# An encoder trunk on one Trainium2 core: half-height score products, turned group-0 values, query norms inside the softmax, and elementwise work taken off GpSimd

## The chip, the core and the metric

The kernel runs on one core of one Trainium2 chip. The metric is the device time of one execution in microseconds (us). The engines are named as in the profile: PE is TensorE with PEld for its weight loads, DVE is VectorE, ACT is ScalarE, POOL is GpSimd, SP is SyncE, which here only issues DMAs. The median of three runs of the kernel before is 1399.47 us (1397.34 to 1400.84).

## What is computed

Two encoder layers work on 512 tokens of 1024 channels, all in float32. One layer, cut to what matters here:

```python
h    = layer_norm(x) * (1 + sc1) + sh1
proj = h @ w_in                       # q,k,v of branch A; q,k,v of branch B; two gates
# A: 8 query heads, 2 key heads, rms-normed per head, rotary; softmax over all 512 keys
qa = rope(rms_norm(qa, qn_g)); ka = rope(rms_norm(ka, kn_g))
out_a = softmax(qa @ ka.T / 8) @ va
# B: three groups of 4 heads, (window, dilation) = (128,1), (512,4), (2048,16), ALiBi bias
o_g, lse_g = dilated_group(qd, kd, vd)          # within the window, every dilation-th key
out_b = sum_g softmax_g(lse_g) * o_g
mix  = (g_a * (out_a @ w_pa) + g_b * (out_b @ w_pb)) @ w_o
x    = layer_norm(ALPHA * x + g1 * mix) * ln1_g + ln1_b
h2   = layer_norm(x) * (1 + sc2) + sh2
x    = layer_norm(ALPHA * x + g2 * moe(h2)) * ln2_g + ln2_b   # 16 experts, top 2 of the best group
```

## The kernel before

Tokens are worked on in four tiles of 128. Products of activations and weights take three passes (`gemm3`, L220): each operand is split into a rounded part H and a remainder L, and H*H, H*L and L*H are added. Weights come by SP's queue; `wsplit` (L195) makes H by an ACT copy (L215) and L by a DVE subtraction (L216). The products of attention and some transposes take plain float32, which stands in the trace as two PE instructions for a product. Each engine runs its instructions in a fixed order that a scheduler draws up at compile time, near the order of the program, with what it expects to be ready first.

The stages of a layer, with their place in layer 0 of the trace:

- Head (to 60 us): the modulation vectors, the normed input turned to channels-first, and its split `apply` (L372): four of eight remainders on POOL (L378). In layer 1 the head is `head_next` (L390), run tile by tile behind the end of layer 0; there POOL makes the remainder of block 3 (L413).
- Rope (94 to 119 us): `rope` (L588) squares and sums the queries and keys of a tile, POOL raises ten sums to the power -1/2 (`pool_rsqrt`, L286), DVE multiplies all 640 columns by the result (L604), ACT and DVE split them, PE turns them (`qk_trans`, L615). Between two tiles stands one product of `fill_b`.
- Branch A (126 to 264 us): 64 units of one head and one tile: score product (L647), maximum (L650), exponential (L653), four transposes, the value product. `fill_b` (L506) puts the projections for branch B between units. The values of group 0 are made there token-major (L527): five blocks of tokens, 24 products of 256 columns each. Those of groups 1 and 2 are made channels-first with 512 columns and turned later by `turned` (L552).
- Branch B (264 to 371 us): 24 units (group, pair of heads `ii`, tile `b`). `b_keys` (L727) copies the keys of two heads by SP's queue into a buffer whose other halves are zero, so that one full-height product (L743) gives both heads' scores. Bias (L745), maximum (L746), exponential (L749), transposes, copy and value product (`b_out`, L753) follow two units later. `fill_g` puts the gate projections in between, one at every second unit.
- Merge (392 to 433 us): `join` (L886), products with w_branch_a and w_branch_b, gating; POOL adds two of four blocks (L916).
- Out (433 to 495 us): `out_block` (L941): output projection by 256 columns, DVE scales (L947), POOL adds into `xr` but for two blocks (L948). `tile_x1` and `tile_h2` norm each tile twice through `norm` (L313): DVE works on 768 columns (896 for h2), ACT and POOL on the others. The h2 of the last tile is finished by ACT and POOL behind the router's sigmoid (L1003 to L1008) and stored by SP's queue.
- Router (495 to 517 us): a chain of small DVE instructions ranks the experts (L1011 to L1076), then POOL gathers token rows by an indirect DMA (`x_load`, L1102) into buffers `xe` that POOL zeroed (L1100).
- Experts (517 to 692 us): 16 experts, `x_gate`, `x_up`, `x_down`.
- Combine (from 692 us): `rows_in` (L1299) adds the experts' rows to x1: four of eight by an ACT scaling (L1303) and a POOL addition (L1304), the others by DVE (L1306). `combine` and `finish` norm each tile (L1341).

Of the kernel before, what the change touches and what calls it, by code (L numbers as in the profile page):

```python
# [87 lines left out]
def build(tc, A, out):  # L88
    nc = tc.nc
    with ExitStack() as es:  # L90
# [222 lines left out]
        def norm(src, name, g, b, st=None, cut=None):  # L313

            cut = cut or CUT
            m, r, nb = st or stats(src)
            n = f4(name, [D])
            for p, z in parts(src, cut, D) if cut < D else []:
                issued["act"] = ACT.activation(n[:, z], p, AF.Identity, bias=nb, scale=r)  # L319
            for p, z in parts(src, 0, cut):  # L320
                V.scalar_tensor_tensor(n[:, z], p, m, g[:, z], op0=OP.subtract, op1=OP.mult)  # L321
            a, z = slice(0, cut), slice(cut, D)
            issued["dve"] = V.scalar_tensor_tensor(n[:, a], n[:, a], r, b[:, a], op0=OP.mult, op1=OP.add)  # L323
            if cut < D:
                PO.tensor_tensor(n[:, z], n[:, z], g[:, z], op=OP.mult)  # L325
                PO.tensor_tensor(n[:, z], n[:, z], b[:, z], op=OP.add)
            return n
# [21 lines left out]
        def head_first(xt):  # L349
# [24 lines left out]
            def apply(k):  # L374
# [3 lines left out]
                (PO if k % 2 else V).tensor_tensor(L, z, H.bitcast(F32), op=OP.subtract)  # L378
# [11 lines left out]
        def head_next(l):  # L390
# [4 lines left out]
            def tile_in(t, x, st):  # L395
# [3 lines left out]
                for q in range(2):  # L399
# [10 lines left out]
                    for j in range(2 * q, 2 * q + 2):  # L410
                        f, H, L = F[:, 2 * j:2 * j + 2, :], hH[j][:, :, tcols(t)], hL[j][:, :, tcols(t)]
                        ACT.copy(H, f)  # L412
                        i = (PO if j in HLP else V).tensor_tensor(L, f, H.bitcast(F32), op=OP.subtract)  # L413
                        if j not in HLP:
                            issued["head"] = i
# [14 lines left out]
        def layer(l, hH, hL, W0, after=None, qk=None):  # L430
# [75 lines left out]
            def fill_b():  # L506
                for g in range(3):
# [16 lines left out]
                    if g == 0:  # L524
                        dst5 = small("vB5", [256], bufs=1)
                        turned()
                        for b in range(5):  # L527
                            p = pmm([P, 256])
                            lo, hi = max(0, P * b - 64), min(S, P * b + 64)
                            m = hi - lo  # L530
                            gemm3(p[0:m, :], range(8), lambda k: hcol(k, slice(lo, hi)), lambda k: W(k, slice(0, 256)))
                            ACT.copy(dst[0:m, b, :] if b < 4 else dst5[0:m, :], p[0:m, :])
                            if b % 2 == 1:
                                yield
                        vB.append((dst, dst5))
                    else:
                        for c in range(2):
                            turned()
                            p = pmm([P, S])
                            gemm3(p, range(8), lambda k: W(k, slice(c * P, (c + 1) * P)),  # L540
                                  lambda k: hcol(k, slice(0, S)))
                            vT = sc("vT", [S])
                            ACT.copy(by_tile(vT, g), by_class(p, g))
                            late.append((vT, dst, c))
                            yield
                        vB.append((dst, None))
# [5 lines left out]
            def turned():  # L552

                while late:
                    vT, dst, c = late.pop(0)
                    p = ptp([P, 4, P])
                    transposes(lambda b: vT[:, tcols(b)], p, 4)
                    V.tensor_copy(dst[:, :, c * P:(c + 1) * P], p)

# [26 lines left out]
            QK = {}  # L586

            def rope(t):  # L588
# [15 lines left out]
                V.tensor_mul(hv(a), hv(a), rs[:, :, None].to_broadcast([P, 10, HD]))  # L604
# [39 lines left out]
            def a_scores(h, t):  # L644
# [5 lines left out]
                V.tensor_reduce(nm, s, axis=X, op=OP.max, negate=True)  # L650
# [73 lines left out]
            for z in kz:  # L724
                PO.memset(z, 0.0)
# [687 lines left out]
```

## Time and profile before

| | us |
|---|---|
| median of three runs | 1399.47 |
| profiled execution | 1398.57 |
| span of its trace | 1396.8 |
| PE busy | 1278.9 |
| DVE busy | 1024.2 |
| ACT busy | 720.2 |
| POOL busy | 282.4 |

A timeline row gives start, duration, engine, line, operation, tile written and tiles read, shape, count, and in brackets the idle time before it with what ended it. Instructions of PE overlap: the pitch, from one start to the next, is what a product costs, not its duration. A row of a table of stretches gives the length, busy time and count for each engine, the granted TensorE clock, the DMA share and GB/s. A row of groups gives busy time and mean ns of one.

### The profile page before, as it was taken

What the parts mean: (1) busy time and instruction counts of PE and PEld (TensorE: products, weight loads), DVE (VectorE), ACT (ScalarE), POOL (GpSimd) and SP (SyncE); (2) the same over time, 40 slices, a digit from 0 to 9 for tenths busy, and PEclk for the clock granted to TensorE, in tenths of its full rate; (3) what the DMA queues carried; (4) which work ended last, traced back from release to release, by engine and by line L of the source; (5) the groups of instructions that cost most, each with busy time, mean ns of one, the idle gap of its engine ahead of it and who ended that gap; (6) DMA issues with size and microseconds to landing.
All of it is one profiled execution on the core that took longest, in us unless ns stands there. A gap on an engine that the chain in (4) does not pass through costs nothing. (4 is left out here: it accounts for less than half of the span.)

```text
span 1396.8 us, 21644 instructions
## 1 busy us (share of the span) xinstructions
PE 1278.9 (92%) x7953; PEld 1039.7 (74%) x7953; DVE 1024.2 (73%) x1974; ACT 720.2 (52%) x1506; POOL 282.4 (20%) x273
## 2 busy tenths in 40 slices
PE   5898999999998949999889999999999894999986
PEld 4797777677777938888659787767777784888862
DVE  5877777767367778999798877564336767899985
ACT  2344444555644237777645444455565522777760
POOL 1132000000002651221341300000000256222224
PEclk9999999999999969999999999999999996999998
DMA  9646654556155187999653555122214536799952
GB/s 317 218 156 239 208 167 167 154 185 218 32 174 204 61 272 260 308 346 338 233 182 125 160 181 170 61 76 76 76 46 151 180 122 218 272 301 344 352 206 84
DMA packets 182992, 266.76 MB, mean 191 GB/s; under 512 B 18665, under 2 KB 131721, under 8 KB 182880
## 3 DMA queue, kind: packets, MB, share of 16 engines
q1 hardware_dynamic: 159312, 225.46, 48.4%
q0 software_dynamic: 11456, 24.07, 4.9%
q10 hardware_dynamic: 12112, 15.78, 3.7%
q8 instruction: 64, 1.05, 0.3%
q14 instruction: 48, 0.39, 0.1%
HBM read 250.79 MB, written 27.30 MB: 199 GB/s over the span
## 5 line engine op out<-in xcount | busy, mean ns | idle before, releaser
L216 DVE TENSOR_TENSOR wL<-raw,wH 128x512 fp32r<-128x512 f32 x520 | 349.9, 703 | 67.3 <-ACT wH L215 52.0
L215 ACT CAST wH<-raw 128x512 fp32r<-128x512 f32 x520 | 318.9, 622 | 148.4 <-PE mm L1175 41.6
L225 PE MATMUL mm<-hH,wH 128*128 128x512 f32 x512 | 206.4, 403 | 0.0
L226 PE MATMUL mm<-hL,wH 128*128 128x512 f32 x512 | 202.4, 395 | 0.0
L227 PE MATMUL mm<-hH,wL 128*128 128x512 f32 x512 | 202.0, 394 | 0.0
L225 PE MATMUL mm<-wH,xH 128*128 128x256 f32 x512 | 149.1, 291 | 1.0 <-ACT xH L343 1.0
L227 PE MATMUL mm<-wH,xL 128*128 128x256 f32 x512 | 148.9, 291 | 0.9 <-DVE xL L344 0.9
L226 PE MATMUL mm<-wL,xH 128*128 128x256 f32 x512 | 146.6, 286 | 0.3 <-DVE wL L216 0.3
L249 DVE SCALAR_TENSOR_TENSOR acc<-araw,cond,acc 128x512 f32<-128x512 f32 x148 | 110.7, 749 | 5.5 <-DMA araw<-in_w_ada 2.3
L227 PEld LDWEIGHTS mm<-hH,wL 128*128 128x128 f32 x512 | 96.2, 188 | 21.1 <-issue 1.1
L225 PEld LDWEIGHTS mm<-hH,wH 128*128 128x128 f32 x512 | 96.3, 188 | 20.1 <-issue 1.2
L226 PEld LDWEIGHTS mm<-hL,wH 128*128 128x128 f32 x512 | 96.3, 188 | 19.1 <-issue 0.3
L225 PEld LDWEIGHTS mm<-wH,xH 128*128 128x128 f32 x512 | 99.0, 193 | 3.1 <-ACT xH L343 2.0
L226 PEld LDWEIGHTS mm<-wL,xH 128*128 128x128 f32 x512 | 98.9, 193 | 2.4 <-DVE wL L216 1.2
L227 PEld LDWEIGHTS mm<-wH,xL 128*128 128x128 f32 x512 | 98.6, 192 | 2.3 <-DVE xL L344 1.8
L225 PE MATMUL mm<-wH,hH 128*128 128x256 f32 (+1 forms) x272 | 81.7, 301 | 4.6 <-ACT hH L412 2.8
L227 PE MATMUL mm<-wH,hL 128*128 128x256 f32 (+1 forms) x272 | 81.2, 300 | 2.1 <-DVE hL L378 0.7
L226 PE MATMUL mm<-wL,hH 128*128 128x256 f32 (+1 forms) x272 | 80.5, 296 | 0.1
L1180 POOL DMA_INDIRECT y<-ye,vt x28 | 33.6, 1202 | 209.8 <-DVE ye L1176 209.8
L281 POOL DMA_DIRECT2D mod<-adar x8 | 4.3, 532 | 331.4 <-ACT adar L280 331.4
L1175 PE MATMUL mm<-raw,eT 128*128 128x512 f32 x128 | 65.4, 635 | 3.6 <-ACT eT L1158 1.5
L745 DVE TENSOR_TENSOR zB<-sB,biasB 128x256 f32<-128x256 f32 (+2 forms) x48 | 22.8, 488 | 61.4 <-PE sB L743 27.7
(316 smaller groups left out, 2873.0 us busy)
## 6 DMA issues: line engine op xcount, KB each, us to landing
araw<-in_w_ada SPq DMA_DIRECT2D x44, 1024.0 KB, 5.3
raw<-in_w_in SPq DMA_DIRECT2D x40, 1024.0 KB, 5.2
raw<-in_w_exp_gate SPq DMA_DIRECT2D x32, 1024.0 KB, 9.3
raw<-in_w_exp_up SPq DMA_DIRECT2D x28, 1024.0 KB, 12.4
raw<-in_w_exp_down SPq DMA_DIRECT2D x28, 1024.0 KB, 10.0
raw<-in_w_out SPq DMA_DIRECT2D x8, 1024.0 KB, 7.2
y<-y SPq DMA_DIRECT2D x16, 512.0 KB, 8.4
eraw<-in_w_ada SPq DMA_DIRECT2D x4, 1024.0 KB, 16.0
```

The costliest lines, as they stand in the source:

```text
L215: ACT.copy(H, raw(s))
L216: V.tensor_sub(L, raw(s), H.bitcast(F32))
L225: PE.matmul(o, lhsT=lH, rhs=rH, start=(i == 0), stop=False)
L226: PE.matmul(o, lhsT=lH, rhs=rL, start=False, stop=False)
L227: PE.matmul(o, lhsT=lL, rhs=rH, start=False, stop=(i == n - 1))
L249: last = V.scalar_tensor_tensor(acc, raw[:, k, :], ck, acc, op0=OP.mult, op1=OP.add)
L281: PO.dma_start(moddr[l, kind].rearrange("o (k n) -> (o k) n", n=P), r[0:8, :])
L745: V.tensor_add(z, s[:, :, 0:wid], biasB[g][:, ii::2, j0:j0 + wid])
L1175: PE.matmul(p, lhsT=a, rhs=w, start=(i == 0), stop=(i == len(todo) - 1))
L1180: st = PO.indirect_dma_start(out=y2, out_offset=bass.IndirectOffsetOnAxis(ap=vidx[:, e:e + 1], axis=0), in_=ye, in_offset=None, bounds_che ...
```

## The change

It has these parts; the diff is cut to its core.

- `norm` has no share for ACT and POOL: DVE subtracts the mean and scales in pieces of columns 0 to 256 and 256 to 1024 (a third piece where the source is two PSUM tiles), then finishes all 1024 in one instruction.
- The other POOL additions and subtractions (L378, L413, L892, L916, L948, L1304) go to DVE; the zeroing (L1026, L1100) goes to ACT as a product with 0.0. What POOL keeps: the powers and `nb` in `stats`, DMAs and the zeros of y2.
- The last tile's h2 is normed like the others and stored by ACT's queue.
- `rope` multiplies the keys alone by their norms; those of a query go into its softmax, as scale of the exponential and into its maximum.
- Group 0's values are made channels-first and turned, like the others'; the tiles are shifted by 64 tokens.
- `b_keys` and its buffers are gone. A score product takes 64 rows, one head; a unit is two tiles, and in groups 1 and 2 four tiles are asked for at once. The two heads go to two PSUM tiles.

```diff
-        def norm(src, name, g, b, st=None, cut=None):
+        def norm(src, name, g, b, st=None):
...
+            for lo, hi in ((0, 256), (256, D)):
+                for p, z in parts(src, lo, hi):
+                    V.scalar_tensor_tensor(n[:, z], p, m, g[:, z], op0=OP.subtract, op1=OP.mult)
+            V.scalar_tensor_tensor(n, n, r, b, op0=OP.mult, op1=OP.add)
...
+                    for c in range(2):
                         turned()
...
+                        p = pmm([P, S])
+                        gemm3(p, range(8), lambda k: W(k, slice(c * P, (c + 1) * P)),
+                              lambda k: hcol(k, slice(0, S)))
+                        vT = sc("vT", [S])
+                        ACT.copy(by_tile(vT, g), by_class(p, g))
+                        late.append((vT, dst, dst5, c))
...
-                V.tensor_mul(hv(a), hv(a), rs[:, :, None].to_broadcast([P, 10, HD]))
+                RS[t] = rs
+                ak = hv(a[:, 512:640])
+                V.tensor_mul(ak, ak, rs[:, 8:10, None].to_broadcast([P, 2, HD]))
...
+                rs = RS[t][:, h:h + 1]
+                V.tensor_mul(nm, nm, rs)
...
-                ACT.activation(pp, s, AF.Exp, bias=nm, accum_out=dn)
+                ACT.activation(pp, s, AF.Exp, bias=nm, scale=rs, accum_out=dn)
...
+            def b_score(s, u, i, g, ii, b, lo, w):
+                r = slice(64 * u, 64 * u + 64)
+                PE.matmul(s[:, i, 0:w], lhsT=qB[g][r, ii, tcols(b)], rhs=kB[g][r, ii, lo:lo + w], start=True, stop=True)
...
+                ss = [pat([P, NT, P], "sB") for _ in range(2)]
+                for b in range(NT):
+                    for u in range(2):
+                        b_score(ss[u], u, b, g, ii, b, P * b, P)
+                z = f4("zB", [NT, 2, P])
+                for u in range(2):
+                    V.tensor_add(z[:, :, u], ss[u], biasB[g][:, ii + 2 * u, None, :].to_broadcast([P, NT, P]))
+                V.tensor_reduce(nmB[:, g, :, ii::2], z, axis=X, op=OP.max, negate=True)
+                for b in range(NT):
+                    b_exp(z[:, b], g, ii, b, P)
...
+            for i in range(len(units) + 1):
+                for u in ask.get(i, []):
+                    b_scores(*u)
+                step(fillg)
...
-                (V if (t, b) in XDVE else PO).tensor_tensor(xr[t][:, cb], xr[t][:, cb], y, op=OP.add)
+                V.tensor_add(xr[t][:, cb], xr[t][:, cb], y)
...
+                n2 = norm(n, "h2", r_sc2, r_sh2, st)
+                (SY if t < NT - 1 else ACT).dma_start(h2d[tcols(t), :], n2)
...
-                    if (t, k) in PROWS[l]:
-                        ACT.mul(y, y, gt[:, k, t:t + 1])
-                        PO.tensor_tensor(x1[t], x1[t], y, op=OP.add)
-                    else:
-                        V.scalar_tensor_tensor(x1[t], y, gt[:, k, t:t + 1], x1[t], op0=OP.mult, op1=OP.add)
+                    V.scalar_tensor_tensor(x1[t], y, gt[:, k, t:t + 1], x1[t], op0=OP.mult, op1=OP.add)
```

## Rows read from the trace of the kernel before

**Rows 1.** The page: busy time of the engines, and PE's share in 40 slices.
```profile
PE 1278.9 (92%) x7953; PEld 1039.7 (74%) x7953; DVE 1024.2 (73%) x1974; ACT 720.2 (52%) x1506; POOL 282.4 (20%) x273
...
PE   5898999999998949999889999999999894999986
```
**Rows 2.** Stretches of layer 0: branch B, second half of merge, out, combine with next head.
```profile
259.50:361.00 101.50, 99.53 (x597) 74.78 (x596) 66.63 (x120) 55.40 (x166) 0.41 (x1) 1.00 0.59 182
...
416.00:433.00 17.00, 14.03 (x66) 10.93 (x64) 15.36 (x23) 9.60 (x15) 4.38 (x3) 1.00 0.26 85
433.00:495.00 62.00, 58.51 (x466) 56.55 (x467) 44.63 (x77) 19.09 (x27) 32.70 (x41) 0.97 0.48 161
...
680.00:741.00 61.00, 50.32 (x218) 32.62 (x217) 47.61 (x92) 29.73 (x63) 27.39 (x32) 0.92 0.60 212
```
**Rows 3.** Timeline of PE: products of 256 columns (values), then of 512 (gates).
```profile
134.13 0.28 PE L227 MATMUL mm<-wH,hL 128*64 128x256 f32 x1
134.25 0.28 PE L225 MATMUL mm<-wH,hH 128*64 128x256 f32 x1
...
390.67 0.39 PE L227 MATMUL mm<-hH,wL 128*128 128x512 f32 x1
390.89 0.39 PE L225 MATMUL mm<-hH,wH 128*128 128x512 f32 x1
```
**Rows 4.** Timeline of PE in branch B of layer 0.
```profile
264.59 0.88 PE L743 MATMUL sB<-kz,qkB 128*128 128x384 f32 x2 [1.94 <-DMA kz<-qkB]
...
278.37 0.81 PE L743 MATMUL sB<-kz,qkB 128*128 128x384 f32 x2
279.02 0.49 PE L336 MATMUL tp<-c_ident,zB 128*128 128x128 f32 x3
279.55 0.66 PE L774 MATMUL ob<-pTB,vB 128*64 128x128 f32 x8
280.14 0.33 PE L336 MATMUL tp<-c_ident,zB 128*128 128x128 f32 x1
```
**Rows 5.** Rope in layer 0: timelines of POOL, DVE and PE, and one stretch.
```profile
99.43 5.08 POOL L286 TENSOR_TENSOR rs<-rs,c_mhalf 128x10 f32<-128x10 f32 x1 [4.82 <-DVE rs L285]
...
104.54 0.83 DVE L604 TENSOR_TENSOR ra<-ra,rs 128x640 f32<-128x640 f32 x1 [1.85 <-POOL rs L286]
...
107.05 0.85 PE L620 MATMUL tp<-identr,q 128*128 128x128 f32 x8 [1.71 <-DVE q L608]
...
116.00:120.00 4.00, 3.45 (x32) 3.35 (x32) 3.23 (x8) 2.27 (x5) 3.43 (x7) 0.57 0.94 314
```
**Rows 6.** Groups by shape: POOL's addition of 256 columns, and a DVE instruction of 256.
```profile
L948 POOL TENSOR_TENSOR xr<-xr,mix 128x256 f32<-128x256 f32 x28 | 20.3, 735 | 37.4 <-DVE mix L947 30.2 <-ACT xr L929 4.5 <-DMA raw<-in_w_exp_gate 2.7
...
L947 DVE TENSOR_TENSOR mix<-mo,row 128x256 f32<-128x256 f32 x32 | 13.1, 414 | 9.1 <-PE mo L227 9.0
```
**Rows 7.** Router of layer 0: one DVE group of its stretch, and SP's and POOL's timeline.
```profile
L1022 DVE TENSOR_TENSOR versus<-rt_sel 128x48 f32<-128x48 f32 x1 | 1.2, 1154 | 0.0
...
504.22 0.34 SPq L1008 DMA_DIRECT2D h2d<-h  x1
...
512.59 1.19 POOL L1106 DMA_INDIRECT xe<-h2d,vt  x1 [5.73 <-DVE rt_we L1197]
```
**Rows 8.** Last expert of layer 0: timelines of POOL and DVE.
```profile
684.30 2.38 POOL L1304 TENSOR_TENSOR x<-x,y 128x1024 f32<-128x1024 f32 x1 [9.14 <-ACT y L1303]
...
684.76 2.47 DVE L216 TENSOR_TENSOR wL<-raw,wH 128x512 fp32r<-128x512 f32 x1 [2.64 <-ACT wH L215]
...
689.90 1.27 DVE L1306 SCALAR_TENSOR_TENSOR x<-y,rt_gt,x 128x1024 f32<-128x1024 f32 x1
691.09 0.41 DVE L1138 TENSOR_TENSOR ea<-ea,mm 128x256 f32<-128x256 f32 x1
```
**Rows 9.** The chain that ended last: start, us, what; two tiles of the last norm.
```profile
1373.75 1.22 DVE st L303 x2
...
1378.62 1.22 DVE st L303 x2
```

More of the change, by code (lines that the diff above doesn't have):

```diff
@@ L412, in tile_in @@
                         ACT.copy(H, f)
-                        i = (PO if j in HLP else V).tensor_tensor(L, f, H.bitcast(F32), op=OP.subtract)
-                        if j not in HLP:
-                            issued["head"] = i
+                        issued["head"] = V.tensor_sub(L, f, H.bitcast(F32))
             return hH, hL, tile_in
@@ L523, in fill_b @@
                     dst = f4("vB", [4, 256])
-                    if g == 0:
-                        dst5 = small("vB5", [256], bufs=1)
+                    dst5 = small("vB5", [256], bufs=1) if g == 0 else None
+                    for c in range(2):
                         turned()
[L527 to L535, printed above, removed]
-                    else:
[L537 to L546, printed above, removed]
+                        p = pmm([P, S])
[4 more added lines that the diff above has]
+                        late.append((vT, dst, dst5, c))
+                        yield
+                    vB.append((dst, dst5))
                     ada_step()
@@ new lines, in b_out2 @@
+            def b_out2(g, ii, b0):
+                zs = [PB.pop((g, ii, b)) for b in (b0, b0 + 1)]
+                if b0 == 0:
+                    OB[g, ii] = pat([P, S], "ob")
+                ob = OB[g, ii]
+                p = ptp([P, 2, 2, P])
+                for i in range(2):
+                    for u in range(2):
+                        turn(p[:, i, u], zs[i][:, u])
+                pT = sc("pTB", [2, 2, P])
+                ACT.copy(pT, p)
+                for i in range(2):
+                    for u in range(2):
+                        c = HD * (u + 2 * ii)
+                        PE.matmul(ob[64 * u:64 * u + 64, tcols(b0 + i)], lhsT=vB[g][0][:, b0 + i, c:c + HD],
+                                  rhs=pT[:, i, u], start=True, stop=True)
+                if b0:
+                    b_keep(g, ii)
@@ L959, in tile_x1 @@
                 r1.append(st[1])
[L960 removed]
+                n = norm(xr[t], "x1", r_g, r_b, st)
                 x1.append(n)
@@ L1096, in layer @@
             XE, XS, WD = {}, {}, {}
-            xes = [f4("xe", [D]) for _ in range(NXE)]
-            for z in xes:
-                PO.memset(z, 0.0)
             def x_load(e):
```

142 lines of the change are left out of this document (57 added, 85 removed).

## The prediction, made before the changed kernel was run

> **What bounds the kernel now.** I read the page first: PE is busy for 1278.9 of 1396.8 us and DVE for 1024.2 [rows 1]. The reader is to see in the slices where PE is not at 9: the head, the out and router stretch around slices 14 and 15, the joint of the layers, the same places of layer 1, and the end. Elsewhere PE sets the pace, and a product that goes is time that goes. Second I read the stretches of one layer. In branch B, PE is busy for 99.53 of 101.50 us, DVE for 66.63. In the second half of the merge it is the other way: DVE 15.36 of 17.00, PE 14.03. In the out stage PE has 58.51 of 62.00 and DVE 44.63, and in the combine stretch DVE has 47.61 of 61.00 [rows 2]. So the change has to be costed by stage: where it takes PE's products away it gains, where it hands POOL's work to DVE it can lose. Third, the timelines give what a product or a wait costs in its place.
>
> The sum is made against the profiled execution's 1398.57 us, 0.9 us below the median of the three runs. About 0.3% (4.2 us) is what a measurement of this kernel can tell from no change.
>
> **Group-0 values** (each layer). Removed: 5 blocks of 24 products of 256 columns, pitch 0.12 [rows 3], 14.4 us. Added: 2 x 24 products of 512 columns at 0.227 (0.22 between the two starts shown, one step of the clock of the table), 10.9 us [rows 3], and 10 transposes of 128 columns. A float32 product of 384 columns takes 0.65 us in its two instructions [rows 4], so one instruction of 128 columns is 0.11 and the transposes are 1.1. Saved: 2.4, both layers 4.8. PE is full there [rows 1], so it counts whole. DVE gains two copies of 512 columns and two small ones, ACT loses five copies for two; both have room between the fills.
>
> **Score products of B** (each layer). Before, group 0 has 2 pairs x (384 + 512 + 512 + 384) columns and groups 1 and 2 have 16 x 256, together 7680 columns. At 0.65 us for 384 [rows 4] that is 13.0 us. Half of each product is zeros. After, the columns per head are the same, but two half-height products stand side by side, 6.5 us if both halves of the array run at once. The trace has no product of 64 rows with a partner in the other rows. The nearest row is that of half-width products: eight instructions of 128 columns, which one after another would take 8 x 0.11 = 0.87, went by in 0.59 (279.55 to 280.14, the change of form included) [rows 4]. So halves of the columns do run at once. Full pairing would save 6.5, the ratio of that row (32%) 4.2; I take 5.2 between them, since after the change a visit holds eight or sixteen instructions and pays its change of form less often per product. Both layers: 10.4. The bounds: 13.0, and a loss of 2.4 if halves of the rows run one after another and each of 16 visits still pays the 0.15 that this row holds over four pairs.
>
> **Keys' copies.** The first score product waited 1.94 us for its padded keys [rows 4]; layer 1 shows no such wait. The copies go, nothing replaces them: 1.9. The maximum over four tiles at once delays the first exponential by less than one gate product, which stands between asking and use.
>
> **Rope** (each layer). The power on ten columns took 5.08 us, DVE then stood 1.85 before L604, and the turning of the queries waited 1.71 behind that [rows 5]. In the stretch from 116 the granted clock was 0.57, so PE ran partly at 1.2 instead of 2.4 GHz after having stood [rows 5]. After the change the queries need no norm: only the keys' multiply (128 instead of 640 columns) waits for POOL, with the query remainder and a weight's remainder queued behind it on DVE if the scheduler puts it first. POOL's power is not made faster. Two waits of 1.7 or more per layer with a slow stretch behind them; I take 2.5 per layer, 5.0 in all, bounds 0 and 12 (both waits, the slow clock and what DVE no longer does). The multiply of the maximum adds 64 one-column DVE instructions before an exponential; two units lie between a score and its use, so it is hidden, and costs under 0.15 each (9 us) if that cover went.
>
> **Merge.** Per layer DVE gets six 512-column additions (join and gates). What goes is POOL's turn and the blocking below. DVE is nearly full here [rows 2]; I take -1.5 for both layers, bounds -3 and +4.
>
> **Out.** Per layer DVE gets 14 additions of 256 columns at 0.41 [rows 6], 5.7 us, and the columns of the norms that ACT and POOL had: in x1 of three tiles 256 in both steps (at most 3 x 0.82), in h2 of three 128, together about 3.5; 9.2 us. It has 17.4 idle there [rows 2], largely waits for POOL, whose addition takes 0.74 against DVE's 0.41 [rows 6]. A tile then needs about as much DVE time as its period is now. I take +1.0 for both layers, bounds -3 and +8.
>
> **Router** (each layer). A small DVE instruction of 48 columns took 1.15 us [rows 7]; the other three like it are the ones that overlap POOL's additions and zeroing, each about 1.0 over its bare time, 2.9 in all. That blocking goes with POOL's work. The last h2 is finished by a 1024-column DVE instruction in front of the ranking, 1.27 by [rows 8], some 0.3 of it under the sigmoid: +1.0. So the indices come 1.9 earlier. The gather at 512.59 followed the storing of h2, issued at 504.22 [rows 7]; that store is now issued behind DVE instead of behind ACT and POOL, about 2 us earlier, by ACT's queue, with the rest of ACT's queue (sigmoid, zeroing) behind it if the scheduler orders it so. ACT's four 1024-column jobs then end before the gather. I take 4.5 for both layers, bounds 2 and 8.
> First the row: 8.4 us from issue to the gather [rows 7]. The Trainium skill, "DMA: Bandwidth & Descriptors", section "Issuing engines are not separate DMA queues", says that DMAs of all issuing engines end on the same 16 engines and interleave, and that another issuer saves only issue time. By that the store would land no sooner for its new queue, only for its earlier issue, and the term would be 4 instead of 4.5.
>
> **Joint of the layers and end.** In the last expert DVE's remainder L216 took 2.47 us, over a POOL addition of 2.38, and another like it; then came L1306, and the expert's product ea, made long before, was only finished at 691.09 [rows 8]. POOL's additions and ACT's scalings go, so ea comes about 4.5 earlier in layer 0 and 3 in layer 1, with two rows of 1.2 in front instead of one. Behind it DVE has three more rows, two of them on the path (2.4). In layer 0 DVE then norms four tiles with 256 more columns in two steps and one more remainder each, about 1.0 a tile, part of it given back by blocking that goes: the joint is -4.5 + 2.4 + 1.1 = -1.0, bounds -6 and +5. At the end a tile takes 4.87 us [rows 9], of which POOL's two small steps and ACT stand between DVE's; after it DVE works without them: two statistics (1.22), small ones 0.4, three pieces 1.35, the finish 1.3, 4.3 us. Four tiles give 2.3, ea 3, less 1.5 for the rows: -4.0 with rounding, bounds -7 and +1. The head loses blocking and gains four remainders: -0.5.
>
> **The sum:** 1398.6 - 4.8 - 10.4 - 1.9 - 5.0 - 1.5 + 1.0 - 4.5 - 1.0 - 4.0 - 0.5 = 1366.0.
>
> **Rivals.**
> *Halves of the rows run one after another.* Against it stand the half-width rows [rows 4]; for it, that no row shows two row halves. Then 10.4 goes and up to 2.4 is added: about 1378.
> *POOL keeps rope and DVE takes the gain back.* The power stays on POOL. It began when DVE had work and ended only 1.85 us after DVE had nothing more to run [rows 5]. If the keys' multiply is put in front of the queries' split, rope gains nothing, and with out and joint at +4 each above my value the time is 1366 + 5 + 8 = 1379. The Trainium skill, "SBUF — State Buffer", section "SBUF: two separate sides", says that DVE instructions with two SBUF inputs and POOL share a port pair as an exclusive lock for a whole instruction. By that rule POOL's powers are held off as before; the trace agrees, in the 5.08 and in the 2.47 over 2.38.
> *PE keeps its clock.* If the waits in rope and merge shrink enough for the slow stretches to go, as that at 0.57 [rows 5], rope gives 12 and the joint 5: about 1354.
> *Slower: DVE becomes the path.* In merge, out, joint and end DVE gets 28 + 12 additions, 8 rows, the norms' columns and the remainders, some 45 us for the kernel. If it had no room there, all of it would lie on the path, against 26.6 of gains elsewhere (values, scores, keys, rope, router): 1398.6 + 45 - 26.6 = 1417. It decides from 59% of the 45 us on the path. Against it: 17.4 us of idle DVE in one out stage [rows 2], and that some of its busy time is waiting for POOL [rows 7, 8].
>
> **How the numbers follow.** My forecast has 0.62, row halves in turn 0.15, rope and DVE 0.12, the clock 0.07, slower 0.04. Two that come together give up to 1391. The range 1350 to 1384 takes in the first four and the spread of the bounds, which partly cancel. Faster by over 0.3% means under 1394.4: 0.94; within 0.3%: 0.03; slower: 0.03.
>
> **What would show it.** Score products of 64 rows should start in pairs a few ns apart, and their column time should halve. The transposes of the queries in rope should follow the addition, not the power. The small DVE instructions of the router should all be near 0.2, and the gather near 509. ea should come within 2 us of its product. Tiles of the last norm should stand 4.3 apart. I would be wrong if the out stage or the joint were longer by over 5 us with DVE full, or if the score products took as long as before.

## The result and the profile after

The changed kernel took 1374.18 us (median of four runs, 1372.27 to 1376.40) beside 1398.40 of the kernel before: a ratio of 0.9822, with a 95% interval of 0.9802 to 0.9842, or 24.9 us (22.1 to 27.7) less. The forecast was 1366.0, 32.6 less. The profiled execution took 1374.85 with a span of 1373.1, 23.7 us under that of before, and the rows below divide these 23.7.

Busy time on the page after, which answers to [rows 1]:

```profile
PE 1262.8 (92%) x7925; PEld 1027.6 (75%) x7925; DVE 1031.9 (75%) x2104; ACT 704.5 (51%) x1460; POOL 157.5 (11%) x161
...
PE   4898999999999949999969899999999994999996
```

PE is busy for 16.1 us less, POOL for 125 less, and DVE for only 7.7 more, although it took over POOL's additions, the norms' columns and the remainders. The DVE instructions that both kernels have in the same number and shape took 28.5 us less in sum, the 520 remainders of L216 alone 9.2: part of what DVE was charged with before was waiting for POOL, as in the 2.47 us row of [rows 8].

The stages, from the first and last starts of their products on PE in the two timelines (layer 0, layer 1; us):

| stage, from PE's start to PE's start | before | after | change, both | forecast |
|---|---|---|---|---|
| head, to the first turned query | 91.7 | 91.7 | 0.0 | -0.5 |
| rope, to the first score of branch A | 35.0, 32.6 | 31.3, 32.8 | -3.5 | -5.0 |
| A and B, to the last value product of B | 244.1, 237.5 | 241.8, 232.2 | -7.6 | -17.1 |
| gates and w_branch_a, to the first product with w_branch_b | 45.8, 45.8 | 45.9, 46.0 | +0.3 | 0 |
| second half of merge | 13.9, 13.9 | 12.2, 12.2 | -3.4 | -1.5 |
| out, to the last logit product | 64.4, 65.0 | 62.8, 62.8 | -3.8 | +1.0 |
| router, to the first turned row of an expert | 22.2, 20.4 | 19.6, 19.5 | -3.5 | -4.5 |
| experts, to the last product of x_up | 168.2, 168.5 | 168.8, 169.7 | +1.8 | 0 |
| joint, to layer 1's first turned query | 85.1 | 89.4 | +4.3 | -1.0 |
| end | 42.7 | 34.5 | -8.2 | -4.0 |

Stages that an edit does not touch also differ between the kernels of this document: the head takes 89.7 to 93.0, layer 1's rope 30.8 to 32.8 with the same instructions, out 62.8 to 64.0 and the joint 87.3 to 90.4, while A and B of layer 1 (232.2), merge (12.2) and the end (34.5) come back within 0.3. Differences inside these spreads show nothing.

The direction and three quarters of the size came as forecast, but not stage by stage: A and B gave 9.5 less than expected and the joint lost 5.3 more, while merge, out and end gave 10.9 more. The stretches after that answer to [rows 2] (length, then PE, PEld, DVE, ACT, POOL busy, granted clock, DMA share, GB/s): second half of merge, out, combine with the next head, end. Their bounds are those of the stage table, which are not those of [rows 2]; the last two rows are out and combine of the kernel before in the table's bounds.

```profile
410.50:422.80 12.30, 11.96 (x50) 8.68 (x48) 12.19 (x21) 7.38 (x12) 0.00 (x0) 1.00 0.32 106
422.80:485.70 62.90, 59.22 (x482) 57.07 (x481) 52.66 (x104) 17.77 (x25) 8.44 (x13) 1.00 0.49 169
...
664.00:731.80 67.80, 52.93 (x220) 35.86 (x218) 53.39 (x106) 24.52 (x55) 7.89 (x16) 0.85 0.54 193
1338.50:1373.00 34.50, 24.24 (x63) 11.13 (x61) 26.30 (x43) 0.65 (x2) 3.26 (x8) 0.90 0.34 138
...
430.40:494.90 64.50, 60.38 (x481) 58.18 (x479) 46.99 (x81) 21.33 (x30) 32.62 (x42) 0.97 0.46 154
...
674.50:738.40 63.90, 52.70 (x236) 34.66 (x234) 52.01 (x98) 32.37 (x66) 28.00 (x32) 0.92 0.59 208
```

**Scores.** Products of 64 rows do start in pairs, 7 ns apart. PE's timeline after, in group 1, answers to [rows 4]:

```profile
318.55 0.60 PE L330 MATMUL tp<-c_ident,zB 128*128 128x128 f32 x4
319.08 0.71 PE L714 MATMUL sB<-qkB 64*128 64x128 f32 x8
319.88 0.66 PE L767 MATMUL ob<-pTB,vB 128*64 128x128 f32 x8
320.46 0.71 PE L714 MATMUL sB<-qkB 64*128 64x128 f32 x8
321.11 0.50 PE L225 MATMUL mm<-hH,wH 128*128 128x512 f32 x1
```

Eight instructions of 128 columns in four pairs would take 4 x 0.11 = 0.44 us at half the column time. They took 0.80 and 0.65 from their start to the next product's. The 0.36 and 0.21 more I put down to changing the form of the array, at each of two visits to one set of scores: the pairs stand 0.11 apart, but the second starts 0.21 behind the first, and the next product 0.35 and 0.20 behind the last pair. There are 24 such visits in the kernel. The intervals behind all score products add up to 26.3 us before (96 instructions) and 21.0 after (192).

**Rope.** The queries no longer wait; the keys do. ACT, DVE and PE after, at the second tile, answering to [rows 5]:

```profile
93.37 0.50 ACT L597 CAST k<-ra 128x128 fp32r<-128x128 f32 x2 [2.12 <-DVE ra L591]
93.77 0.59 ACT L509 ACTIVATE qkB<-mm 128x512 f32<-128x512 f32 x1
94.26 1.06 ACT L608 CAST qT<-tp 128x512 fp32r<-128x512 f32 x2
...
93.04 0.29 DVE L591 TENSOR_TENSOR ra<-ra,rs 128x128 f32<-128x128 f32 x1 [1.85 <-POOL rs L286]
93.25 0.69 DVE L595 TENSOR_TENSOR q<-ra,q 128x512 fp32r<-128x512 f32 x1
...
94.89 0.54 PE L611 MATMUL tp<-identr,k 128*128 128x128 f32 x4 [1.90 <-ACT qT L608]
...
96.00:100.00 4.00, 4.00 (x12) 3.12 (x11) 3.89 (x11) 1.24 (x2) 3.37 (x1) 0.57 0.00 0
```

On ACT the keys' cast of this tile (L597) stands in front of the copy that frees PSUM of the tile before (L608). It waits for the keys' multiply, that for POOL's power, and PE's turning of the older keys waits 1.90 us for the copy. In the stretch behind it the granted clock is 0.57, mostly the lower of its two levels (1.2 GHz), as in [rows 5]. On DVE the keys' multiply (L591) stands in front of the queries' split (L595), as the second rival had it.

**A weight in layer 0.** PE now comes, by way of DVE, to a weight of branch A that has only just landed (SP's queue, ACT, DVE, PE):

```profile
123.78 0.37 SPq L192 DMA_DIRECT2D raw<-in_w_in  x1
...
133.40 1.14 ACT L215 CAST wH<-raw 128x512 fp32r<-128x512 f32 x2 [5.59 <-DMA raw<-in_w_in]
...
134.05 1.29 DVE L216 TENSOR_TENSOR wL<-raw,wH 128x512 fp32r<-128x512 f32 x2 [5.35 <-ACT wH L215]
...
136.53 0.15 DVE L273 SCALAR_TENSOR_TENSOR mc<-adap,bcol 128x4 f32<-128x4 f32 x1
...
136.74 0.27 PE L278 MATMUL tp<-c_ident,mc 128*8 128x128 f32 x1 [3.60 <-DVE mc L273]
```

Its load was issued at 123.78 and landed 9.5 us later, while 4 MB of zeros for the experts' rows went through the same DMA engines. PE does not wait for the weight itself: the small column mc, which it turns next, stands behind the weight's remainders in DVE's order. Before, the load took 11.0 us (125.92 to 136.88), and PE came to mc at 138.32 without a wait.

**Joint.** DVE, SP's queue, PE and two stretches after, answering to [rows 8]:

```profile
674.42 0.42 DVE L1151 TENSOR_TENSOR ea<-ea,mm 128x256 f32<-128x256 f32 x1 [0.24 <-PE mm L227]
...
680.23 4.87 DVE L1315 SCALAR_TENSOR_TENSOR x<-y,rt_gt,x 128x1024 f32<-128x1024 f32 x4
688.08 2.50 DVE L216 TENSOR_TENSOR wL<-raw,wH 128x512 fp32r<-128x512 f32 x4 [2.98 <-ACT wH L215]
690.49 1.88 DVE L303 BATCH_NORM_STATS2 st<-y 128x6 f32<-128x512 f32 x3
...
674.86 12.62 SPq L192 DMA_DIRECT2D raw<-in_w_in  x4
...
694.01 3.59 PE L1321 MATMUL y<-yk,G 128*128 128x512 f32 x4 [5.99 <-DVE rstd L285]
...
690.00:694.00 4.00, 0.00 (x0) 0.00 (x0) 4.00 (x12) 1.14 (x2) 0.71 (x2) 0.56 1.09 352
694.00:698.00 4.00, 3.99 (x6) 1.84 (x7) 4.00 (x8) 0.00 (x0) 0.91 (x3) 0.59 0.83 313
```

ea starts as soon as its product is there (DVE was idle for 0.24 us in front of it) and is finished at 674.8. But now the next layer's weight is late: it lands at 687.4, 12.5 us after its issue at 674.86 (the row's 12.62 is the time over which four loads were issued); four of its remainders (L216) stand on DVE in front of the statistics of the first tile, and until these are read PSUM isn't free for the third tile's products. PE stands for 5.99 us, and behind that its granted clock is 0.59, mostly the lower level (1.2 GHz).

**Router and end.** The instruction of [rows 7] that took 1.15 (L1022, now L1041) takes 0.24, like its neighbour, and the gather starts at 500.64, 15.0 us after the last logit product instead of 17.7. It follows the landing of the last store of h2 by 0.9 us (1.0 in layer 1); the DVE instruction that its row names is another one in layer 1:

```profile
492.90 0.24 DVE L1040 TENSOR_TENSOR versus<-rt_sel 128x48 f32<-128x48 f32 x1
493.19 0.24 DVE L1041 TENSOR_TENSOR versus<-rt_sel 128x48 f32<-128x48 f32 x1
...
500.64 1.17 POOL L1119 DMA_INDIRECT xe<-h2d,vt  x1 [9.25 <-DVE rt_we L1210]
```

### The profile page after: what moved, and what is told of

It is laid out like the page before. It is cut to its first block, busy times and chain, and to the rows that moved or that the text cites. A ratio compares the mean times of both kernels' runs of the same rounds, so it can differ in the third digit from the quotient of the medians.

```text
span 1373.1 us, 21373 instructions
## 1 busy us (share of the span) xinstructions
PE 1262.8 (92%) x7925; PEld 1027.6 (75%) x7925; DVE 1031.9 (75%) x2104; ACT 704.5 (51%) x1460; POOL 157.5 (11%) x161
## 4 chain that ended last, share of the span: by engine, by line
PE 32%; DVE 10%; ACT 2%; issue 2%; DMA 2%; POOL 1%; SPq 1%; POOLq 0%; DVEq 0%; ACTq 0%
PE mm L225 5%; PE mm L226 5%; PE mm L227 5%; DVE wL L216 5%; PE mm L1188 3%; PE tp L330 2%; PE av L668 1%; PE y L1321 1%; ACT wH L215 1%; POOL rs L286 1%; PE mo L226 1%; PE mo L227 1%; PE mo L225 1%; PE s L634 1%; DMA raw<-in_w_exp_down 1%
## 5 line engine op out<-in xcount | busy, mean ns | idle before, releaser
L216 DVE TENSOR_TENSOR wL<-raw,wH 128x512 fp32r<-128x512 f32 x520 | 339.7, 685 | 94.4 <-ACT wH L215 80.6
L215 ACT CAST wH<-raw 128x512 fp32r<-128x512 f32 x520 | 318.4, 622 | 163.5 <-PE mm L1188 45.9
L225 PE MATMUL mm<-hH,wH 128*128 128x512 f32 x544 | 219.3, 403 | 0.0
L226 PE MATMUL mm<-hL,wH 128*128 128x512 f32 x544 | 217.9, 400 | 0.0
L227 PE MATMUL mm<-hH,wL 128*128 128x512 f32 x544 | 216.1, 397 | 0.0
L227 PEld LDWEIGHTS mm<-hH,wL 128*128 128x128 f32 x544 | 103.4, 190 | 21.2 <-issue 0.7
L286 POOL TENSOR_TENSOR rstd<-rstd,c_mhalf 128x1 f32<-128x1 f32 x32 | 20.4, 637 | 478.1 <-DVE rstd L285 478.1
L642 ACT ACTIVATE pp<-s,nm,rs 128x512 f32<-128x512 f32 x64 | 49.7, 778 | 33.0 <-DVE nm L639 31.3
L225 PE MATMUL mm<-wH,hH 128*128 128x256 f32 x192 | 58.7, 308 | 5.4 <-ACT hH L406 3.6
L227 PE MATMUL mm<-wH,hL 128*128 128x256 f32 x192 | 57.2, 303 | 1.6 <-DVE hL L372 1.4
L226 PE MATMUL mm<-wL,hH 128*128 128x256 f32 x192 | 56.7, 299 | 0.0
```

The lines of the kernel that those rows point to most:

```text
L215: ACT.copy(H, raw(s))
L216: V.tensor_sub(L, raw(s), H.bitcast(F32))
L225: PE.matmul(o, lhsT=lH, rhs=rH, start=(i == 0), stop=False)
L226: PE.matmul(o, lhsT=lH, rhs=rL, start=False, stop=False)
L227: PE.matmul(o, lhsT=lL, rhs=rH, start=False, stop=(i == n - 1))
L286: PO.tensor_tensor(r, r, mhalf[:, :n], op=OP.pow)
```

## The experiments

Ratios are to the kernel before, run beside each; the changed kernel has 0.9822 (0.9802 to 0.9842). Intervals of about 0.002 each way are 3 us, so where two kernels are closer than that, the lengths of the stages that the edit touches decide, as far as they exceed the spreads above.

**One part undone at a time.** Full-height scores with key copies, in units of one tile:

```diff
-                PE.matmul(s[:, i, 0:w], lhsT=qB[g][r, ii, tcols(b)], rhs=kB[g][r, ii, lo:lo + w], start=True, stop=True)
...
+                PE.matmul(s[:, :, 0:wid], lhsT=qB[g][:, ii, tcols(b)], rhs=rk, start=True, stop=True)
```

> The changed kernel with one part undone: the scores of branch B come from full-height products with padded keys again, unit by unit, the key copies with them. What the traces say so far: the intervals behind the score products add up to 26.3 us before and 21.0 after (both layers), so halves of the rows do run at once, but a change of form is paid at every visit. By that theory this kernel takes 5.3 us more than the changed one, and up to 1.9 more for the wait for padded keys: 1379 to 1381 us, ratio to before 0.986 to 0.988. By the prediction as it stands (10.4 and 1.9) it takes 12 more: 1386. By the rival that the time saved on PE is taken by something else in branch B (its stretch in layer 0 shrank by 0.7 only) it takes within 2 of the changed kernel: 1374 to 1376.

Measured: 0.9874 (0.9853 to 0.9896), 7.3 us more than the changed kernel. A and B took 246.4 and 237.5 instead of 241.8 and 232.2, 9.9 more, of which the waits for padded keys were 1.87 and 1.15. The joint, which the edit does not touch, is 1.6 shorter here. By the total the first theory is right. Of the 9.9 the keys take 3.0 (predicted 1.9) and the products and what stands around them 6.9, of which the intervals behind the score products, 26.0 here, show 5.0.

Group 0's values token-major:

```diff
-                        gemm3(p, range(8), lambda k: W(k, slice(c * P, (c + 1) * P)), lambda k: hcol(k, slice(0, S)))
...
+                            gemm3(p[0:m, :], range(8), lambda k: hcol(k, slice(lo, hi)), lambda k: W(k, slice(0, 256)))
```

> The changed kernel with one part undone: the values of group 0 are made token-major in five blocks again, nothing is turned. By the prediction (PE is full in branch A, the time of the products counts whole) it takes 4.8 us more: 1379. By the rival it takes 2.4 more, since in layer 0 PE waits 3.6 us for a weight right behind these products, and products that take longer only shorten that wait: 1376 to 1377.

Measured: 0.9801 (0.9777 to 0.9826); both expectations missed, for undoing this part cost nothing. In layer 1 A and B were 2.0 longer (234.2), as the products say. In layer 0 they were 1.9 shorter (239.9): the wait of 3.60 is not in this trace. There PE comes to mc at 134.25, where it stood from 133.1 on in the changed kernel, and DVE has mc (133.79) in front of the remainders that start at 134.26. This reads as a real gain that was lost behind the weight; whether that holds is tested below.

Rope with all norms:

```diff
-                ak = hv(a[:, 512:640])
-                V.tensor_mul(ak, ak, rs[:, 8:10, None].to_broadcast([P, 2, HD]))
+                V.tensor_mul(hv(a), hv(a), rs[:, :, None].to_broadcast([P, 10, HD]))
...
```

> The changed kernel with one part undone: rope multiplies all ten heads by their norms again, the softmax has no norm. By the theory from the trace after, the wait has only moved from the queries to the keys: PE's waits at the transposes add up to 7.7 us before (four of them) and 5.9 after (four), and layer 0's gain ran into the wait for a weight. Then this kernel is within 2 us of the changed one: 1373 to 1376. By the prediction it takes 5.0 more: 1379. By the rival that the 64 small multiplies per layer cost more than the wait, it takes 2 or more less: 1372 or below.

Measured: 0.9849 (0.9826 to 0.9872), 3.8 more, nearer to the prediction's 5.0 than to my newer theory. Rope took 34.5 and 31.0 against 31.3 and 32.8. Layer 1's difference lies in its spread: with this rope or the old one a second wait of some 2 us is there in some kernels and not in others. In layer 0 the three kernels with the old rope took 34.5 to 35.0 and the seven with the changed one 30.9 to 33.0, so the gain is in layer 0.

Only POOL's elementwise work taken away, all else as before (one of the lines, against the kernel before):

```diff
-                    if (t, k) in PROWS[l]:
-                        ACT.mul(y, y, gt[:, k, t:t + 1])
-                        PO.tensor_tensor(x1[t], x1[t], y, op=OP.add)
-                    else:
-                        V.scalar_tensor_tensor(x1[t], y, gt[:, k, t:t + 1], x1[t], op0=OP.mult, op1=OP.add)
+                    V.scalar_tensor_tensor(x1[t], y, gt[:, k, t:t + 1], x1[t], op0=OP.mult, op1=OP.add)
```

> The kernel before with only the elementwise work taken off POOL (norm, head, merge, out, last h2, zeroing, combine); rope, values and scores as before. By the stage lengths of the two traces (merge -3.4, out -3.9, router -3.6, experts +1.8, joint +4.4, end -8.1) it takes 12.8 us less than before: 1385 to 1386, ratio 0.991. By the terms of the prediction (-1.5 +1.0 -4.5 -1.0 -4.0 -0.5) it takes 10.5 less: 1388. By the rival that DVE becomes the path it is no faster than before: 1396 or more. Together with the three kernels that undo one part each it also tells whether the parts add up.

Measured: 0.9889 (0.9863 to 0.9915), 15.5 us less than before (12 to 19), more than the 12.8 of the traces and the prediction's 10.5. DVE did not become the path: it is busy for 13.2 us more than before. The joint is 88.3, so the joint's loss comes with this part. With scores (7.3), values (-2.9) and rope (3.8) the sum is 23.7, beside 24.9 measured: the parts add up, as far as terms tell that are each uncertain by 3 us.

**Waits that replaced waits.** At the joint, the split of the next layer's first weight behind the statistics of tile 1 on DVE:

```diff
-            W0 = w_block(l + 1, 0) if nxt else None
+            raw0 = wraw(A["w_in"][l + 1][:, 0:256]..., [8, 256]) if nxt else None
...
+                if nxt and i == 1:
+                    W0 = wsplit(raw0, [8, 256], behind=[issued["bn"]])
```

> The changed kernel with one order altered at the joint of the layers: the split of layer 1's first weight block stands behind the statistics of tile 1 on DVE instead of ahead of those of tile 0; its load is issued as before. Theory: after the change DVE has its rows done at 685.1 but stands at four weight remainders whose weight only lands at 687.4, the statistics that would free PSUM stand behind them, and PE waits 5.99 us. Then this order gives 4 to 5 us: ratio to before 0.979, 1369 to 1371 against 1374 to 1375, and the wait at the third tile falls under 1.5. Rival: the joint is set by the amount of DVE's work (DVE 53.4 of 67.8 us there), then the wait only moves behind the next tile: under 1 us, 1373 to 1375.

Measured: 0.9778 (0.9764 to 0.9793), 6.2 less. The joint is 83.0 instead of 89.4, shorter than before the change. DVE, PE and a stretch of this kernel:

```profile
681.02 4.86 DVE L1315 SCALAR_TENSOR_TENSOR x<-y,rt_gt,x 128x1024 f32<-128x1024 f32 x4
685.80 1.29 DVE L303 BATCH_NORM_STATS2 st<-y 128x6 f32<-128x512 f32 x2
...
692.78 1.12 PE L1321 MATMUL y<-yk,G 128*128 128x512 f32 x2 [1.41 <-DVE xo L319]
...
694.00:698.00 4.00, 4.00 (x10) 1.59 (x9) 4.00 (x11) 0.00 (x0) 0.60 (x2) 1.00 1.06 387
```

The statistics follow the rows at once; the weight landed no sooner and is no longer in the way. The wait at the third tile is shorter by 4.6 us; the rest fits the clock, which stays at 1.00 where it was 0.59. The order caused the wait, not the amount of DVE's work.

In rope, the keys' multiply behind the split of the queries and the keys' casts behind the copies of the tile before:

```diff
+            def rope_k(t, behind):
...
+                with ExitStack() as es:
+                    for z in order + behind:
+                        es.enter_context(tc.issue_after(z.ins))
+                    V.tensor_mul(ak, ak, RS[t][:, 8:10, None].to_broadcast([P, 2, HD]))
+                    for e in range(2):
+                        ACT.copy(k2[:, 0, :, e, :], hv(a[:, 512:640]))
```

> The changed kernel with one order altered in rope: the keys' multiply of a tile stands behind the split of its queries and the copies of the tile before on DVE, and the keys' casts behind the copies of the tile before on ACT. Theory: after the change PE waits 1.90 + 0.39 + 1.56 + 2.01 us at the keys' transposes since ACT's copies out of PSUM stand behind casts that wait for POOL's power; in this order these waits go: 4 to 6 us less, 1369 to 1371. Rival: the power is still the last to come, and the waits turn up at the keys' own transposes one step later, or at the first scores: within 1 us, 1373 to 1376.

Measured: 0.9804 (0.9790 to 0.9818), 2.5 less, short of the 4 to 6. Rope itself gave more than expected, 27.5 in both layers (-3.8, -5.3), but A and B of layer 0 took 244.6 instead of 241.8. PE of this kernel there:

```profile
136.93 0.38 PE L278 MATMUL tp<-c_ident,mc 128*8 128x128 f32 x1 [6.62 <-DVE mc L273]
```

The weight lands when it did, and PE only comes to it earlier: of rope's 3.8 in layer 0 the wait took back 3.0. The edit moves instructions on DVE and on ACT; what each order is worth was not run apart.

The zeros written in branch B of layer 0:

```diff
-                zero = f4("zero", [D])
-                PO.memset(zero, 0.0)
...
+                if l == 0 and i == 10:
+                    zero = f4("zero", [D])
+                    ACT.mul(zero, oB[1].rearrange("p a b -> p (a b)"), 0.0)
```

> The changed kernel with the 4 MB of zeros for the experts' rows written during the second half of branch B of layer 0 instead of at the start of branch A (their source is made by ACT there). Theory: at 133.4 a weight lands 9.5 us after its issue, since the zeros fill the DMA engines, ACT waits 5.6 and PE 3.6 us for it; that ate the gain of rope and values in layer 0. Then 3 to 4 us less: 1370 to 1371, ratio 0.979 to 0.980. Rival: the next weight is late by as much, or the zeros hold up w_branch_a: within 1 us, 1373 to 1376.

Measured: 0.9784 (0.9767 to 0.9800), 5.3 less. A and B of layer 0 took 237.5 (-4.3), and PE has no wait over 0.8 us in branch A. ACT's cast of the weight starts 5.1 us after the load was issued (at 123.01):

```profile
128.13 1.21 ACT L215 CAST wH<-raw 128x512 fp32r<-128x512 f32 x2 [1.08 <-DMA raw<-in_w_in]
```

The zeros were what made the weight late.

**The out stage.** Additions into xr on POOL again:

```diff
-                V.tensor_add(xr[t][:, cb], xr[t][:, cb], y)
+                (V if (t, b) in ((3, 2), (3, 3)) else PO).tensor_tensor(xr[t][:, cb], xr[t][:, cb], y, op=OP.add)
```

> The changed kernel with one piece undone: the additions into xr in the out stage are POOL's again (but for the last two blocks). By the traces (out 64.4 and 65.0 us before, 62.8 and 62.8 after) POOL's addition is on the way of every tile's transposes, 0.74 and more against 0.41 on DVE, and slows DVE's own: 3 to 4 us more, 1377 to 1379, ratio 0.984 to 0.985. By the prediction, which put +1.0 there for DVE's added work, about 1 less: 1373. Rival: other pieces of the change (norms on DVE alone) made the gain, the additions nothing: 1374 to 1375.

Measured: 0.9822 (0.9808 to 0.9837), no change. Out took 62.9 and 63.4, the changed kernel 62.8 and 62.8. My theory fell; the rival was right about the additions.

Norm columns given to ACT and POOL again (768 of 1024 on DVE, 896 for h2):

```diff
+            for p, z in parts(src, cut, D) if cut < D else []:
+                ACT.activation(n[:, z], p, AF.Identity, bias=nb, scale=r)
...
+                PO.tensor_tensor(n[:, z], n[:, z], g[:, z], op=OP.mult)
+                PO.tensor_tensor(n[:, z], n[:, z], b[:, z], op=OP.add)
```

> The changed kernel with one piece undone: the norms of x1, h2 and xo give columns to ACT and POOL again (768 or 896 for DVE), the last tile's h2 and all else as changed. The out stage is 1.6 and 2.3 us shorter than before the change, and POOL's additions are not the reason. Theory: the norms are: out longer by 1.5 to 2.3 in each layer, and the end longer by 2 to 4 (its four tiles took 19.6 us before and 17.7 after, the last store ended 1.8 later): 1379 to 1382, ratio to before 0.985 to 0.988. By the prediction DVE's added columns cost 3.5 in an out stage and the tiles of the end gain 2.3 in all: 1374 to 1375. Rival: neither, within 1 of the changed kernel in out, and the end +2.

Measured: 0.9795 (0.9775 to 0.9815), 3.8 less, against all three expectations in the whole; of the 4.5 us by which its span is shorter, 2.0 lie in the head (89.7), which the edit does not touch. The end was 3.8 longer (38.3), as the theory said, but out took 61.5 and 61.8 (1.3 and 1.0 shorter) and the joint 85.2 (4.2 shorter, 2.1 below the spread of the others). So norms on DVE alone cost something in out and joint, as the prediction had it for out, and pay at the end. With both on POOL, as before the change (a kernel that differs in other parts too), out takes 64.4 and 65.0; with the additions alone there 62.9 and 63.4; with the norms alone 61.5 and 61.8; with neither 62.8 and 62.8. So the gain in out comes from POOL no longer doing both, and with either one left to it the gain stays. In layer 1 the trace of before bears this out, with PE's waits of 1.33 and 1.32 us for POOL's addition, which are in neither kernel at that size; in layer 0 the same waits are 0.43 and 0.53 us, and how the two delay each other there stays open.

**All three orders together**, the diffs of the joint, rope and the zeros in one kernel:

> The changed kernel with the three altered orders together (joint: split behind the statistics; rope: keys' casts behind the copies; zeros written in branch B of layer 0). Theory: the three gains add up, and more, since in the kernel with rope's order alone the wait for a weight in layer 0 grew from 3.60 to 6.62 us, which the moved zeros take away: -6.2 (joint), -3.8 and -5.3 (rope by layer), -4.3 (zeros) against the changed kernel: 1354 to 1357, ratio to before 0.967 to 0.970. Rival: after two of them the next wait sets the time (DVE at the joint, the weights' DMA), and the third gives nothing: 1360 to 1364.

Measured: 1357.53 us, 0.9705 (0.9684 to 0.9727), faster than both kernels, some 16 us (1.2%) under the changed one and 0.5 above the range expected. Rope took 27.7 and 27.6, A and B 237.4 and 232.2, the joint 83.8. The gains add up.

On top of these, group 0's values token-major, with the diff shown for them above:

> The kernel with the three altered orders, and the values of group 0 made token-major in five blocks as before the change. With the waits for the weight and in rope gone, theory: the turned values are worth what their products take less, 2.4 us by the prediction and 2.0 by layer 1's stretch, in each layer; this kernel takes 4 to 5 us more than that with the three orders alone. Rival: the turned values gain nothing also here (transposes and copies cost what the products save), within 1.5.

Measured: 0.9727 (0.9704 to 0.9750); by the ratio 3.1 us more than with the three orders alone. A and B took 239.8 and 234.2, that is 2.4 and 2.0 more. The turned values are worth about what the prediction said, once nothing waits behind them.

On top of the three orders, score products kept together, behind the value products in progress:

```diff
...
+                    with ExitStack() as order:
+                        if 'ob' in issued:
+                            order.enter_context(tc.issue_after(issued["ob"].ins))
                         b_scores(*u)
```

> The kernel with the three altered orders, and the score products of a call behind the value products in progress on PE, so that they are not divided: 7 visits to the half-height form in a layer instead of 12. Theory: each visit costs 0.33 us over half the column time (first pair and the change back) and 0.1 on the way in, so ten visits fewer take 3 to 4 us off the intervals behind and before the score products, which fall from 21.0 to under 18.5; the time falls by 2 to 4. Rival: the pairs themselves are slower than half of a full-height product, then the intervals stay above 20 and the time within 1.

Measured: 0.9699 (0.9678 to 0.9720), no different from the three orders alone, so the 2 to 4 expected did not come. The intervals behind the score products did fall, from 21.0 to 16.6 with 14 visits instead of 24, which gives the price of a visit: 4.4 for ten. PE of this kernel, the same group as above, and a wait that it brought:

```profile
310.44 0.66 PE L770 MATMUL ob<-pTB,vB 128*64 128x128 f32 x8
311.03 1.16 PE L717 MATMUL sB<-qkB 64*128 64x128 f32 x16
312.12 0.50 PE L226 MATMUL mm<-hL,wH 128*128 128x512 f32 x1
...
349.83 0.66 PE L770 MATMUL ob<-pTB,vB 128*64 128x128 f32 x8 [2.42 <-ACT pTB L766]
```

Sixteen instructions took 1.09 (0.87 at half the column time) where two visits of eight took 1.45. Layer 1's A and B gained 1.3 (230.9), layer 0's lost 2.2 (239.6), largely in that wait for ACT.

## Why the prediction was right, and where its steps were not

**Sign and size.** The forecast rested on PE's products in A and B and on POOL's blocking elsewhere. Taking POOL's work away gave 15.5 where its terms said 10.5; scores, keys, values and rope gave 8 to 9 where they said 22. Two errors of opposite sign met inside the range, and that the total came so near is luck to that extent. Of the signs named, the pairs, the router's 0.24 us, ea behind its product and the tiles of the last norm (4.4 us apart on average) came. The gather came 2.7 us earlier behind the last logit product, where 509 meant 3.6, and the time of the score products did not halve.

**Values:** -4.8, right as a price (4.4 in A and B with the waits gone), wrong as a gain. The step that failed is "PE is full there, so it counts whole": full before, but in layer 0 a weight that landed 9.5 us after its issue, with mc behind its remainders on DVE, came right after.

**Scores:** -10.4, of which 5.3 came in the intervals. That halves of the rows run at once was right, so the first rival (1378) is out. The term was mis-sized in what I put down to the change of form: I took 0.15 from rows with half-width products and thought that more products at a visit would pay it less often; it is 0.2 to 0.4 at each visit, and the scheduler divided a call's products over two visits. The Trainium skill, "TensorEngine Tiling (Array Packing)", section "Key Properties", says that changing the tiling mode drains the engine; the trace agrees in that time is lost at each visit, 0.36 and 0.21 us around eight instructions, 0.22 around sixteen. The keys' copies were 1.9 in layer 0 as said; in the kernel that has them again layer 1 waits too, 1.15.

**Rope:** -5.0, came as -3.5 to -3.8, cut short by the mechanism of the second rival. The power stayed on POOL at 5.08 us, DVE still stood 1.85 behind it, and the keys' multiply did stand in front of the queries' split. The rival named DVE's queue; the row that PE waited for was a copy in ACT's, behind casts that wait for that multiply. The step that failed is that only the keys' multiply would wait for POOL, with nothing but DVE's queue behind it: ACT's casts waited for that multiply, and behind them the copy that frees PSUM of the tile before. Of layer 0's gain the weight then took a part. With the order mended rope gave 12.3 (35.0 to 27.7 and 32.6 to 27.6), the upper bound of 12, and the granted clock stayed at 1.00 through it, so the third rival's mechanism exists, but needed an edit that the change did not make.

**Merge:** -1.5, came as -3.4, 0.4 beyond the bound; PE is busy for 11.96 of 12.30 us there now. **Out:** +1.0, came as -3.8, also beyond its bound of -3. DVE's added work is 5.7 us in layer 0 (46.99 to 52.66 in the same bounds), where I said 9.2, and a part of it does count: with the norms back on POOL out is 1.0 to 1.3 shorter. Wrong was to put nothing against it for POOL: its additions and norms together had made the stage some 3 us longer than the norms alone do, and in layer 0 the clock of the stage went from 0.97 to 1.00. **Router:** -4.5, came as -3.5, 2.6 in layer 0 and 0.9 in layer 1. The last store of h2 was issued at 492.70 and the gather started 7.9 us later, against 8.4 in [rows 7]; in layer 1, whose rows the prediction did not use, it was 7.9 against 6.8. So the new queue saved nothing here, the earlier issue did.

**Joint:** -1.0, came as +4.3, inside its bounds. ea came as forecast. The step that failed was to end the sum there, at DVE's rows, without asking which transfer the earlier work would meet: the weight's load is issued behind 4 MB of rows, lands 12.5 us after its issue, DVE's fixed order put its remainders first, and PE's clock fell behind the wait. **End:** -4.0 (its terms add up to -3.8), came as -8.2, beyond its bound of -7. From the last product of x_up to the first statistics it was 3.8 less (14.7 to 10.9; I had ea's 3 less 1.5 for the rows), from there to the last store 2.5 less (20.2 to 17.7; I had 2.3), and 1.8 came behind the last store, in no term of mine: the last section says from what.

**Slower:** DVE as the path (1417) is out: I counted 45 us for DVE, and it is busy for 7.7 more, and for 13.2 more where POOL's work alone is moved.

## What to carry to other kernels

When a stage gets faster, look at what stands next in each engine's fixed order: here three gains ran into a weight, a cast and a split that had been hidden, and moving those instructions, with no work removed, gave another 1.2%. A product on half of the array's rows is worth half the time only if many of them stand together; count the visits, not the columns. An engine that is busy because it waits for another (DVE for POOL) has more room than its busy time says, but an undone part tells its worth only in a kernel where nothing else waits behind it.

## What was unexpected of the hardware

In these kernels the program ends a fixed time after POOL's last instruction, not after the last store. From the issue of the last store to the end of the span it was 7.8 us in the kernel before (1389.0 to 1396.8) and in the one with POOL's norm columns (1360.8 to 1368.6), and 5.9 in the other twelve, among them the changed kernel (1367.1 to 1373.1). From the end of POOL's last instruction it was 7.8 us in all fourteen. In the kernel with POOL's norm columns that instruction is an addition, which ends as the store is issued. In the changed kernel it is a small one of the statistics, which ends at 1365.28, 1.9 us before the store:

```profile
1359.43 1.34 POOL L325 TENSOR_TENSOR xo<-xo,row 128x256 f32<-128x256 f32 x1
...
1360.79 0.33 SPq L1356 DMA_DIRECT2D out<-xo  x1
...
1365.02 0.26 POOL L308 TENSOR_SCALAR nb<-mv,rstd 128x1 f32<-128x1 f32 x1
...
1367.14 0.33 SPq L1351 DMA_DIRECT2D out<-xo  x1
```

Within the 7.8 us POOL's queue holds a DRAIN that the timeline leaves out. It ends 7.0 us after POOL's last instruction (at 1372.24 in the changed kernel), and the end of the span follows 0.8 us behind it, while SP's queue was done with its own at 1370.3. So of the end's gain 1.8 us came with POOL's last addition gone from behind the last tile. What the drain waits for was not tested.
